# Two pauses of a recurrence, and the shape of the last token tile in a down projection (one Trainium2 core)

## The chip, the cores and the metric

The kernel runs on one core of one Trainium2 chip. The metric is device time in microseconds (us) of one launch. The engines are called by the short names of the profile: PE is TensorE (matmul), PEld its weight loads, DVE is VectorE, ACT is ScalarE, POOL is GpSimd, SP is SyncE, which here issues most of the DMA transfers.

## The reference

One layer of a hybrid backbone is computed twice: for 128 prompt tokens, and for 512 sample tokens that also read cached context (keys, values, recurrent states). The model width is 1024, the inner width of the feed-forward part 2816. Everything is float32.

```python
def token_mixers(h, lw, ...):
    proj = h @ lw['w_in']                      # 13 pieces, each 256 wide
    y_a = a_b * dwconv3(a_c * a_x, ...)
    y_b, s_f, s_b = hgrn2_bidir(b_q, b_ff, b_fb, b_i, b_g, ...)   # gated linear recurrence, both directions
    y_c = neighbourhood_attention(...)         # for the prompt: context_attention
    y_d = chunk_gmlp(d_u, d_v, ...)
    merged = g_a * (y_a @ w_br_a) + g_b * (y_b @ w_br_b) + g_c * (y_c @ w_br_c) + g_d * (y_d @ w_br_d)
    return merged @ lw['w_o'], kh, vh, s_f, s_b

def trunk_layer(x, cvec, lw, ...):
    mod = silu(cvec) @ lw['w_ada'] + lw['b_ada']                  # adaLN: sh1, sc1, g1, sh2, sc2, g2
    h = rmsnorm(x, norm1_g) * (1 + sc1) + sh1
    x = x + g1 * token_mixers(h)
    h = rmsnorm(x, norm2_g) * (1 + sc2) + sh2
    return x + g2 * conv_ffn(h)                # (silu(g) * a) @ w_down, a and g from dwconv3(h @ w_up)

y_prompt, y_sample = rmsnorm(xp, final_norm_g), rmsnorm(xs, final_norm_g)
```

The change touches the order of `hgrn2_bidir`'s work and the product with `w_down`, with the residual and the final norm behind it.

## The kernel before, in words

**Tiles.** The 640 tokens are five tiles of 128, four of samples and one of the prompt. Nearly all matrix products go through split numbers: a float32 operand is cut into a high and a low part, and a product is three matmuls (high by high, high by low, low by high). TensorE's stream is thus a long row of weight loads and matmuls with 320 or 512 moving columns. For the weights the high part is made by ScalarE (`act`, L310) and the low part by VectorE (L311).

**Who sets the order.** The program is written out in Python by an emitter that keeps a planner's clock, `now[0]`. Each stage of the main stream (`tick(us)`) adds its estimated length to that clock, and then resumes every background job whose due time has come. A background job is a Python generator: the recurrence `hgrn` (started behind the query section, with a slack factor of 1.3), the attention, the gMLP, the adaLN column steps `ada_cols`. At `yield x` a job is put off by x times its slack factor, counted from the clock as it stood before that step. Inside a step `pe(us)` adds the length of the matmuls that the step itself emits. Where an instruction is passed to `tc.keep_in_program_order`, its engine keeps it in the written order; between the others a scheduler chooses the order on each engine.

**The recurrence.** `hgrn` works through seven levels (`for l in range(7)`, L508). At level l it forms the products between neighbouring blocks of 2^l tokens. From level 1 on each level has two bursts, `par` 0 and 1, one for each half of the partitions: for levels 1 to 5 a burst is ten tokens' pieces i by four groups g, 40 products, written as 80 matmuls of 64 rows by 32 columns in the profile (L526), with `pe(0.18)` behind each piece. Between the bursts stands a pause (`yield 0.4`, L537), behind the level the updates of the running products (L545, L549) and a closing pause (`yield HD[1]`, L550, 5). While the bursts run, the main stream is the input projection (L362), 320 columns to a matmul. Levels 0 to 4 write into one buffer, which at the end of level 4 is copied out by ScalarE (L541).

**The down projection.** It works in two halves of the output columns (`nh`), 512 columns each, and in 11 steps (`kk_`) of 256 rows of `w_down`. `down_prep` makes the weight parts and the activations' parts of a step, `down_tile` its matmuls (L1795): for each of the five token tiles two row blocks by three products. Each tile has an accumulator in PSUM. In the second half the steps 8, 9 and 10 are held back and done together, tile by tile, so that each tile's output can follow while the next tile is computed. Before the change the last token tile (t = 4, the prompt) of the second half is computed in two halves of 256 columns in all 11 steps, each in an accumulator of its own.

`down_out` (L1799 to L1832) takes a finished accumulator to the output: VectorE multiplies by the gain g2 (L1806) and adds the residual (L1809); ScalarE squares with a running sum (L1812 in the first half, L1817 in the second); VectorE joins the sums of squares (L1818); GpSimd takes the root (`pow`, L1822); ScalarE scales the first 512 columns (L1824), VectorE the last 512 (L1825), and SyncE sends the row out (L1827). None of these is pinned by `keep_in_program_order`.

Of the kernel before, what the change touches and what calls it, by code (L numbers as in the profile page):

```python
# [15 lines left out]

P = 128
HD = [4, 5, 2.1, 7, 2.2, 1.4, 1.5, 5, 2.0, 2, 11]
OUTS = 1
NPAIR = 22  # L20
BRIDGE = 4
LORD = "0 8 w00 w10 w20 1 9 2 10 3 11 w01 w11 w21 4 5 12 13"
# [45 lines left out]
def tile_step(ctx: ExitStack, tc: tile.TileContext, a: dict, outs: list, dbg=None):  # L68
# [54 lines left out]
    def nm(s):  # L123
        cnt[0] += 1
        return f"{s}_{cnt[0]}"
# [321 lines left out]
    def hgrn():  # L447
# [51 lines left out]
        for l in range(7):  # L499
            B = 1 << l  # L500
            e_, x_ = blk(kk[:, 0], B), blk(kk[:, 1], B)
            r_, p_ = blk(qq[:, 0], B), blk(qq[:, 1], B)
            f_, g_ = blk(ff[:, 0], B), blk(ff[:, 1], B)
            nb = 1280 // (2 * B)
            if l == 0:
                m = yield from along(near)
                vec.copy_predicated(nat, lmask[:, 0, :].unsqueeze(1).to_broadcast([P, 20, 32]), bc(m))

            W = 64 if l == 6 else 32
            ns = 320 // W  # L510
            for s0, par in ([(s_, r) for s_ in range(0, 10, ns) for r in range(2)] if l else ()):
                b = slice(64 * par, 64 * par + 64)
                m = pm()
                for i in range(s0, s0 + ns):
                    for g in range(P // W):
                        d, t0 = (0, W * g) if l < 5 else (1 - g % 2, W * (g ^ 1))
                        t0 += (i % 5) * P
                        k0 = i * P + W * g
                        rhs = qq[b, d, i // 5, t0:t0 + W]
                        if l < 5:  # L520
                            lhs = kl[b, k0:k0 + W]
                            rhs = bass.AP(rhs.tensor, rhs.offset,
                                          [list(rhs.ap[0]), [2 * B, 16 // B], [1280 + B, 2], [1, B]])
                        else:
                            lhs = f2(kk[:, g % 2])[b, k0:k0 + W]
                        mm(m[W * g:W * g + W, (i - s0) * W:(i - s0 + 1) * W], lhs, rhs,  # L526
                           start=True, stop=True, tile_position=(64 * par, W * g))
                    pe(0.18)
                mv = m[:, 0:ns * W].rearrange("p (i t) -> p i t", t=W)
                if l < 5:  # L530
                    vec.copy_predicated(near_at[:, par], lmask[:, l, :].unsqueeze(1).to_broadcast([P, 10, 32]), mv)
                else:
                    for g in range(P // W):
                        c = slice(W * g, W * g + W)
                        act(at[c, par, s0:s0 + ns, W * (g ^ 1):W * (g ^ 1) + W], mv[c], AF.Copy)
                if par == 0:
                    yield 0.4  # L537
            if l == 4:
                for g in range(4):
                    c = slice(32 * g, 32 * g + 32)  # L540
                    act(at[c, :, :, c].rearrange("p r i t -> p (r i) t"), nat[c], AF.Copy)  # L541
            ups = ((e_[:, :, 0, :], f_[:, :, 1, 0:1]), (x_[:, :, 1, :], g_[:, :, 0, 0:1]),
                   (p_[:, :, 1, :], f_[:, :, 0, 0:1]), (r_[:, :, 0, :], g_[:, :, 1, 0:1]))
            for i, (dst, mul) in enumerate(ups):
                vec.tensor_tensor(dst, dst, mul.to_broadcast([P, nb, B]), ALU.mult)  # L545
                if i == 1 and l < 4:
                    kl = keys(l + 1)
            fa = ff.rearrange("p d n t -> p (d n t)").rearrange("p (n j i) -> p n j i", j=2, i=B)
            vec.tensor_tensor(fa[:, :, 0, 0], fa[:, :, 0, 0], fa[:, :, 1, 0], ALU.mult)  # L549
            yield HD[1]  # L550
        vec.tensor_copy(tot, ff.rearrange("p d n (t s) -> p d n t s", s=P)[:, :, :, :, 0])
        R["tots"] = True

# [1211 lines left out]
    def down_tile(nh, kk_, ws):  # L1765
# [7 lines left out]
        if kk_ == 0:  # L1773
            if nh == 0:
                g0, g1, m0 = pg(), pg(), pm()
                acc[0] = [g0[:, 0, :], g0[:, 1, :], g1[:, 0, :], g1[:, 1, :], m0]
            else:
                ms = [pm(), pm(), pm()]
                g0, g1 = pg(), pg()
                acc[1] = ms + [g0[:, 0, :], g1[:, 0, :], pm()]  # L1780
        batch = [ws]
        if nh == 1 and kk_ >= 8:
            acc.setdefault("hold", []).append(ws)
# [2 lines left out]
            batch = acc["hold"]  # L1786
        last = kk_ == 10
        for t in range(5):

            halves = ((0, 256), (256, 512)) if nh == 1 and t == 4 else ((0, 512),)  # L1790
            for c0, c1 in halves:
                for bi, (w, sl) in enumerate(batch):
                    for k in range(2):
                        for i, (hx, hw) in enumerate(((0, 0), (0, 1), (1, 0))):
                            mm(acc[nh][t + c0 // 256][:, 0:c1 - c0], sl[k][hx][:, t * P:(t + 1) * P], w[:, hw, k, c0:c1],  # L1795
                               start=(kk_ == 0 and k == 0 and i == 0),
                               stop=(last and bi == len(batch) - 1 and k == 1 and i == 2))
                        tick(0.65 * (c1 - c0) / 512)
                if last:  # L1799
                    down_out(nh, t, c0, c1)  # L1800

    def down_out(nh, t, c0, c1):
        v = 0 if t < 4 else 1
        cs = slice(nh * 512 + c0, nh * 512 + c1)
        tmp = gp.tile([P, 512], F32, tag="gt", name=nm("dt"))[:, 0:c1 - c0]
        vec.tensor_tensor(tmp, acc[nh][t + c0 // 256][:, 0:c1 - c0], grows["g2"][:, v, cs], ALU.mult)  # L1806
        xs = x2[t][:, cs]
        fg = fx["fn"][:, 1280:2304]
        vec.tensor_tensor(xs, xs, tmp, ALU.add)  # L1809
        q = st3[:, t:t + 1]  # L1810
        if nh == 0:
            act(tmp, xs, AF.Square, accum_out=q)  # L1812
            pool.tensor_tensor(xs, xs, fg[:, cs], ALU.mult)
            vec.tensor_scalar(q, q, 1.0 / D, EPS, ALU.mult, ALU.add)
            return
        q1 = st3[:, 8 + t:9 + t]
        act(tmp, xs, AF.Square, accum_out=q1)  # L1817
        vec.scalar_tensor_tensor(q, q1, 1.0 / D, q, ALU.mult, ALU.add)  # L1818
        if c1 < 512:
            return  # L1820
        r_ = st3[:, 16 + t:17 + t]
        pool.tensor_tensor(r_, q, neghalf[:, 0:1], ALU.pow)  # L1822
        dst = y_sample[0, t * P:(t + 1) * P, :] if t < 4 else y_prompt[0]
        act(x2[t][:, 0:512], x2[t][:, 0:512], AF.Copy, scale=r_)  # L1824
        vec.scalar_tensor_tensor(x2[t][:, 512:], x2[t][:, 512:], r_, fg[:, 512:], ALU.mult, ALU.mult)  # L1825
        if OUTS == 1 or t < 4:
            nc.sync.dma_start(dst, x2[t])  # L1827
        else:
            nc.sync.dma_start(dst[:, 0:512], x2[t][:, 0:512])
            nc.scalar.dma_start(dst[:, 512:], x2[t][:, 512:])  # L1830

    for nh in range(2):  # L1832
        for kk_ in range(11):
# [339 lines left out]
```

## Time and profile before

| what | value |
|---|---|
| median of 3 runs (lowest to highest) | 1027.42 us (1027.24 to 1028.08) |
| the profiled execution's own time | 1028.79 us |
| its span, first to last instruction | 1026.9 us |
| mean granted TensorE clock | 0.996 of full speed |
| busy: VectorE | 792.3 us, 77% of the span, 1300 instructions |
| busy: ScalarE | 535.5 us, 52% of the span, 927 instructions |
| moved by DMA | 177.87 MB, mean 173 GB/s |

A row of the timeline has the start in us from the span's start, the length in us, the engine, the line of the kernel, the operation, the output and inputs by the program's names with partitions x elements, and how many such instructions in a row it stands for (x73). In brackets stands the idle time of the engine just before, in us, and what ended it; "issue" is idle time in which the engine waited for nothing that the profile shows. Matmuls overlap, so the start to start distance is the time that one costs. A row of the table of waits gives who waited for what, then the total, the number of times and the longest. A row of the table of stretches gives for a stretch A:B its length, then the busy time and the number of instructions of each engine, the mean granted TensorE clock (PEclk), the busy share of the DMA engines and the rate moved. A row of a queue gives packets, MB, and the share of the 16 DMA engines' time.

### The profile page before, as it was taken

What the parts mean: (1) busy time and instruction counts of PE and PEld (TensorE: products, weight loads), DVE (VectorE), ACT (ScalarE), POOL (GpSimd) and SP (SyncE); (2) the same over time, 40 slices, a digit from 0 to 9 for tenths busy, and PEclk for the clock granted to TensorE, in tenths of its full rate; (3) what the DMA queues carried; (4) which work ended last, traced back from release to release, by engine and by line L of the source; (5) the groups of instructions that cost most, each with busy time, mean ns of one, the idle gap of its engine ahead of it and who ended that gap; (6) DMA issues with size and microseconds to landing.
All of it is one profiled execution on the core that took longest, in us unless ns stands there. A gap on an engine that the chain in (4) does not pass through costs nothing.

```text
span 1026.9 us, 18833 instructions
## 1 busy us (share of the span) xinstructions
PE 1013.4 (99%) x7620; PEld 957.8 (93%) x7620; DVE 792.3 (77%) x1300; ACT 535.5 (52%) x927; POOL 106.2 (10%) x149
## 2 busy tenths in 40 slices
PE   8999999999999999999999999999999999999997
PEld 6899999999899999999998899999999999888886
DVE  6658889679965676767768879998888887797634
ACT  6642343444444444544544567777777776633332
POOL 1000010313100000000010111111112211001101
PEclk9999999999999999999999999999999999999999
DMA  9864333598562413323179584765555669974212
GB/s 354 319 220 127 125 108 121 137 270 268 121 205 78 137 69 103 127 79 103 41 276 359 200 333 109 192 167 150 149 150 149 156 161 274 366 248 149 89 35 103
DMA packets 55927, 177.87 MB, mean 173 GB/s; under 512 B 8192, under 2 KB 14624, under 8 KB 53280
## 3 DMA queue, kind: packets, MB, share of 16 engines
q1 hardware_dynamic: 45008, 140.60, 39.5%
q0 software_dynamic: 10832, 36.06, 14.7%
q8 instruction: 60, 0.98, 0.4%
q14 instruction: 27, 0.22, 0.1%
HBM read 134.93 MB, written 25.46 MB: 156 GB/s over the span
## 4 chain that ended last, share of the span: by engine, by line
PE 96%; DMA 1%; ACT 1%; DVE 1%; issue 1%; SPq 0%; POOL 0%; POOLq 0%; DVEq 0%; ACTq 0%
PE g L1464 19%; PE g L362 17%; PE m L1108 17%; PE g L1795 8%; PE m L1795 6%; PE g L1121 5%; PE m L1464 4%; PE m L1248 3%; PE g L920 2%; PE g L1248 2%; PE m L148 2%; PE g L148 1%; PE m L526 1%; PE m L1459 1%; DMA A<-in_w_ada_dram 1%; PE m L851 1%
## 5 line engine op out<-in xcount | busy, mean ns | idle before, releaser
L362 PE MATMUL g<-XH,w 128*128 128x320 f32 x704 | 171.9, 319 | 0.0
L362 PEld LDWEIGHTS g<-XH,w 128*128 128x128 f32 x704 | 121.6, 190 | 2.2 <-issue 1.2
L362 PE MATMUL g<-XL,w 128*128 128x320 f32 x352 | 109.8, 312 | 0.0
L362 PEld LDWEIGHTS g<-XL,w 128*128 128x128 f32 x352 | 66.9, 190 | 0.3 <-issue 0.2
L311 DVE TENSOR_TENSOR w<-raw,w 128x1024 fp32r<-128x1024 f32 x34 | 41.5, 1222 | 21.4 <-ACT w L310 15.2
L1108 PE MATMUL m<-XH,w 128*128 128x320 f32 x224 | 52.5, 309 | 0.0
L1795 PE MATMUL g<-w,XH 128*128 128x512 f32 (+1 forms) x216 | 47.6, 373 | 0.0
L310 ACT ACTIVATE w<-raw 128x1024 fp32r<-128x1024 f32 x34 | 35.7, 1050 | 21.3 <-PE g L1248 9.9
L1795 PEld LDWEIGHTS g<-w,XH 128*128 128x128 f32 x216 | 38.4, 188 | 7.6 <-ACT XH L1758 0.3
L148 DVE SCALAR_TENSOR_TENSOR X<-MG,p2t,X 128x641 f32<-128x641 f32 x44 | 38.9, 885 | 4.3 <-ACT X L148 3.4
L148 DVE SCALAR_TENSOR_TENSOR X<-X,p2t,X 128x641 f32<-128x641 f32 x44 | 38.9, 885 | 1.9 <-ACT X L148 1.0
L1795 PE MATMUL g<-w,XL 128*128 128x512 f32 (+1 forms) x180 | 39.8, 372 | 0.0
L148 ACT ACTIVATE w<-raw 128x1024 fp32r<-128x1024 f32 (+3 forms) x46 | 38.2, 850 | 2.9 <-DMA raw<-in_w_in_dram 2.0
L1795 PE MATMUL m<-w,XH 128*128 128x512 f32 (+1 forms) x180 | 39.7, 368 | 0.0
L1464 PE MATMUL g<-XL,w 128*128 128x320 f32 x240 | 38.6, 310 | 0.0
L1464 PE MATMUL g<-XL,C 128*128 128x320 f32 x240 | 38.4, 309 | 0.0
L1795 PEld LDWEIGHTS g<-w,XL 128*128 128x128 f32 x180 | 32.3, 188 | 6.5 <-DVE dt L1806 0.4
L1108 PEld LDWEIGHTS m<-XH,w 128*128 128x128 f32 x224 | 38.3, 188 | 0.0
L1464 PEld LDWEIGHTS g<-XL,w 128*128 128x128 f32 x240 | 36.0, 188 | 0.5 <-ACT MG L148 0.3
L1464 PEld LDWEIGHTS g<-XL,C 128*128 128x128 f32 x240 | 35.9, 188 | 0.4 <-ACT MG L148 0.4
L1795 PEld LDWEIGHTS m<-w,XH 128*128 128x128 f32 x180 | 31.3, 189 | 5.3
L1108 PE MATMUL m<-XL,w 128*128 128x320 f32 x112 | 34.6, 309 | 0.0
(546 smaller groups left out, 2764.5 us busy)
## 6 DMA issues: line engine op xcount, KB each, us to landing
raw<-in_w_up_dram SPq DMA_DIRECT2D x30, 512.0 KB, 5.2
raw<-in_w_gp_dram SPq DMA_DIRECT2D x21, 640.0 KB, 3.9
raw<-in_w_down_dram SPq DMA_DIRECT2D x22, 512.0 KB, 4.0
raw<-in_w_in_dram SPq DMA_DIRECT2D x19, 512.0 KB, 4.1
H<-in_w_adt_dram SPq DMA_DIRECT2D x16, 512.0 KB, 4.3
actd<-X POOLq DMA_DIRECT2D x22, 320.5 KB, 5.5
X<-in_w_adt_dram SPq DMA_DIRECT2D x10, 512.0 KB, 4.4
upd<-XL SPq DMA_DIRECT2D x4, 1280.0 KB, 6.5
```

The source lines that it names most:

```text
L148: r = f(*args, **kw)
L310: act(w[0], raw, AF.Copy)
L311: vec.tensor_tensor(w[1], raw, w[0].bitcast(F32), ALU.subtract)
L362: mm(o, w[:, h, k0 + k, :], r(k)[:, s], start=(k == 0 and i == 0), stop=(k == kt - 1 and i == 2))
L526: mm(m[W * g:W * g + W, (i - s0) * W:(i - s0 + 1) * W], lhs, rhs, start=True, stop=True, tile_position=(64 * par, W * g))
L851: mm(mo[64 * hh_:64 * hh_ + 64, 0:P], v, ptt[(u + hh_) % 3][:, j * P:(j + 1) * P], start=(j == 0), stop=(j == 2))
L920: mm(o, x(kx)[:, ts], w[:, h, k, :], start=(kx == 0 and i == 0), stop=(kx == 7 and i == 2))
L1108: mm(o, w[:, k, :], x[:, k, :], start=(first and k == 0 and j == 0), stop=(k == 3 and j == 2), skip_group_check=True)
L1121: mm(pb[:, c, 0:HC], w[:, h + k, :], y[:, x, k, s], start=(k == 0 and j == 0), stop=(k == 1 and j == 2))
L1248: mm(m, mh[k // 2][:, hx, k % 2, t * P:(t + 1) * P], wo[q][:, hw, k % 2, :], start=(k == 0 and i == 0), stop=(k == 7 and i == 2))
L1464: z = mm(o, w[:, k, :], x[:, k, :], start=(first and k == 0 and j == 0), stop=(k == 3 and j == 2), skip_group_check=True)
L1795: mm(acc[nh][t + c0 // 256][:, 0:c1 - c0], sl[k][hx][:, t * P:(t + 1) * P], w[:, hw, k, c0:c1], start=(kk_ == 0 and k == 0 and i == 0), st ...
```

## The change

In the recurrence, the pause between the two bursts of level 4 is 1.6 instead of 0.4, and the closing pause behind level 4 is 3.8 instead of 5. The other levels keep theirs.

In the second half of the down projection, the last token tile is computed whole (512 columns) for steps 0 to 7, in one accumulator. After step 7 that accumulator is emptied: multiplied by the gain, and added to the residual (`gained`, `added`). The held steps 8 to 10 are computed in two halves of 256 columns as before, in two fresh accumulators (`acc["halves"]`).

`down_out` is cut into pieces (`gained`, `added`, `down_root`, `down_store`), and for the last two halves VectorE's order is written out: the first half's multiply and add; the output of token tile 3; then the second half's multiply, the join of the first half's sum of squares, the second half's add, its square, and its join. The second half's square moves from ScalarE to VectorE. The root is written in place. The constant `OUTS`, which chose between two ways of sending the last row out, is gone; the way that it chose stays.

```diff
@@ -16,7 +16,6 @@
 
 P = 128
 HD = [4, 5, 2.1, 7, 2.2, 1.4, 1.5, 5, 2.0, 2, 11]
-OUTS = 1
 NPAIR = 22
 BRIDGE = 4
 LORD = "0 8 w00 w10 w20 1 9 2 10 3 11 w01 w11 w21 4 5 12 13"
@@ -534,7 +533,7 @@
                         c = slice(W * g, W * g + W)
                         act(at[c, par, s0:s0 + ns, W * (g ^ 1):W * (g ^ 1) + W], mv[c], AF.Copy)
                 if par == 0:
-                    yield 0.4
+                    yield 1.6 if l == 4 else 0.4
             if l == 4:
                 for g in range(4):
                     c = slice(32 * g, 32 * g + 32)
@@ -547,7 +546,7 @@
                     kl = keys(l + 1)
             fa = ff.rearrange("p d n t -> p (d n t)").rearrange("p (n j i) -> p n j i", j=2, i=B)
             vec.tensor_tensor(fa[:, :, 0, 0], fa[:, :, 0, 0], fa[:, :, 1, 0], ALU.mult)
-            yield HD[1]
+            yield HD[1] - (1.2 if l == 4 else 0)
         vec.tensor_copy(tot, ff.rearrange("p d n (t s) -> p d n t s", s=P)[:, :, :, :, 0])
         R["tots"] = True
 
@@ -1775,9 +1774,11 @@
                 g0, g1, m0 = pg(), pg(), pm()
                 acc[0] = [g0[:, 0, :], g0[:, 1, :], g1[:, 0, :], g1[:, 1, :], m0]
             else:
+
                 ms = [pm(), pm(), pm()]
                 g0, g1 = pg(), pg()
-                acc[1] = ms + [g0[:, 0, :], g1[:, 0, :], pm()]
+                acc[1] = ms + [g0[:, 0, :], g0[:, 1, :]]
+                acc["halves"] = [g1[:, 0, :], pm()]
         batch = [ws]
         if nh == 1 and kk_ >= 8:
             acc.setdefault("hold", []).append(ws)
@@ -1786,48 +1787,80 @@
             batch = acc["hold"]
         last = kk_ == 10
         for t in range(5):
-
-            halves = ((0, 256), (256, 512)) if nh == 1 and t == 4 else ((0, 512),)
-            for c0, c1 in halves:
+            halved = last and nh == 1 and t == 4
+            for ci, (c0, c1) in enumerate(((0, 256), (256, 512)) if halved else ((0, 512),)):
+                ps = (acc["halves"][ci] if halved else acc[nh][t])[:, 0:c1 - c0]
                 for bi, (w, sl) in enumerate(batch):
                     for k in range(2):
                         for i, (hx, hw) in enumerate(((0, 0), (0, 1), (1, 0))):
-                            mm(acc[nh][t + c0 // 256][:, 0:c1 - c0], sl[k][hx][:, t * P:(t + 1) * P], w[:, hw, k, c0:c1],
-                               start=(kk_ == 0 and k == 0 and i == 0),
-                               stop=(last and bi == len(batch) - 1 and k == 1 and i == 2))
+                            first = (kk_ == 0 or halved and bi == 0) and k == 0 and i == 0
+                            end = k == 1 and i == 2 and bi == len(batch) - 1
+                            mm(ps, sl[k][hx][:, t * P:(t + 1) * P], w[:, hw, k, c0:c1],
+                               start=first, stop=end and (last or nh == 1 and t == 4 and kk_ == 7))
                         tick(0.65 * (c1 - c0) / 512)
                 if last:
-                    down_out(nh, t, c0, c1)
-
-    def down_out(nh, t, c0, c1):
-        v = 0 if t < 4 else 1
+                    down_out(nh, t, c0, c1, ps)
+        if nh == 1 and kk_ == 7:
+            gained(1, 4, 0, 512, acc[1][4])
+            added(1, 4, 0, 512)
+
+    keep_ = tc.keep_in_program_order
+    prods = {}
+
+    def gained(nh, t, c0, c1, ps):
+
+        tmp = prods[t] = gp.tile([P, 512], F32, tag="gt", name=nm("dt"))[:, 0:c1 - c0]
+        return vec.tensor_tensor(tmp, ps, grows["g2"][:, 0 if t < 4 else 1, nh * 512 + c0:nh * 512 + c1], ALU.mult)
+
+    def added(nh, t, c0, c1):
+        xs = x2[t][:, nh * 512 + c0:nh * 512 + c1]
+        return vec.tensor_tensor(xs, xs, prods[t], ALU.add)
+
+    def down_out(nh, t, c0, c1, ps):
         cs = slice(nh * 512 + c0, nh * 512 + c1)
-        tmp = gp.tile([P, 512], F32, tag="gt", name=nm("dt"))[:, 0:c1 - c0]
-        vec.tensor_tensor(tmp, acc[nh][t + c0 // 256][:, 0:c1 - c0], grows["g2"][:, v, cs], ALU.mult)
         xs = x2[t][:, cs]
-        fg = fx["fn"][:, 1280:2304]
-        vec.tensor_tensor(xs, xs, tmp, ALU.add)
-        q = st3[:, t:t + 1]
+        q, q1, q2 = (st3[:, i + t:i + t + 1] for i in (0, 8, 16))
+        join = lambda x: vec.scalar_tensor_tensor(q, x, 1.0 / D, q, ALU.mult, ALU.add)
         if nh == 0:
-            act(tmp, xs, AF.Square, accum_out=q)
-            pool.tensor_tensor(xs, xs, fg[:, cs], ALU.mult)
+            gained(nh, t, c0, c1, ps)
+            added(nh, t, c0, c1)
+            act(prods[t], xs, AF.Square, accum_out=q)
+            pool.tensor_tensor(xs, xs, fx["fn"][:, 1280:2304][:, cs], ALU.mult)
             vec.tensor_scalar(q, q, 1.0 / D, EPS, ALU.mult, ALU.add)
-            return
-        q1 = st3[:, 8 + t:9 + t]
-        act(tmp, xs, AF.Square, accum_out=q1)
-        vec.scalar_tensor_tensor(q, q1, 1.0 / D, q, ALU.mult, ALU.add)
-        if c1 < 512:
-            return
-        r_ = st3[:, 16 + t:17 + t]
-        pool.tensor_tensor(r_, q, neghalf[:, 0:1], ALU.pow)
+        elif t < 4:
+            gained(nh, t, c0, c1, ps)
+            added(nh, t, c0, c1)
+            act(prods[t], xs, AF.Square, accum_out=q1)
+            join(q1)
+            down_root(t)
+            if t < 3:
+                down_store(t)
+        elif c0 == 0:
+
+            keep_(gained(nh, t, c0, c1, ps))
+            keep_(added(nh, t, c0, c1))
+            down_store(3)
+            keep_(act(prods[t], xs, AF.Square, accum_out=q1))
+        else:
+            keep_(gained(nh, t, c0, c1, ps))
+            keep_(join(q1))
+            keep_(added(nh, t, c0, c1))
+            keep_(vec.scalar_tensor_tensor(prods[t], xs, 1.0, xs, ALU.mult, ALU.mult, accum_out=q2))
+            keep_(join(q2))
+            down_root(4)
+            down_store(4)
+
+    def down_root(t):
+        pool.tensor_tensor(st3[:, t:t + 1], st3[:, t:t + 1], neghalf[:, 0:1], ALU.pow)
+
+    def down_store(t):
         dst = y_sample[0, t * P:(t + 1) * P, :] if t < 4 else y_prompt[0]
-        act(x2[t][:, 0:512], x2[t][:, 0:512], AF.Copy, scale=r_)
-        vec.scalar_tensor_tensor(x2[t][:, 512:], x2[t][:, 512:], r_, fg[:, 512:], ALU.mult, ALU.mult)
-        if OUTS == 1 or t < 4:
-            nc.sync.dma_start(dst, x2[t])
-        else:
-            nc.sync.dma_start(dst[:, 0:512], x2[t][:, 0:512])
-            nc.scalar.dma_start(dst[:, 512:], x2[t][:, 512:])
+        xs = x2[t][:, 512:]
+        act(x2[t][:, 0:512], x2[t][:, 0:512], AF.Copy, scale=st3[:, t:t + 1])
+        m = vec.scalar_tensor_tensor(xs, xs, st3[:, t:t + 1], fx["fn"][:, 1280 + 512:2304], ALU.mult, ALU.mult)
+        if t > 2:
+            keep_(m)
+        nc.sync.dma_start(dst, x2[t])
 
     for nh in range(2):
         for kk_ in range(11):
```

## The prediction, made before the changed kernel was run

> **What bounds the kernel now.** I read the page's head first, then the chain that ended last, then TensorE's waits, then the stretches that the change touches.
>
> ```profile
> span 1026.9 us, 18833 instructions
> ...
> PE 1013.4 (99%) x7620; PEld 957.8 (93%) x7620; DVE 792.3 (77%) x1300; ACT 535.5 (52%) x927; POOL 106.2 (10%) x149
> ...
> PE 96%; DMA 1%; ACT 1%; DVE 1%; issue 1%; SPq 0%; POOL 0%; POOLq 0%; DVEq 0%; ACTq 0%
> ```
>
> TensorE is busy in 99% of the span and is 96% of the chain that ended last. An edit therefore counts if it shortens TensorE's own stream, if it takes away one of that engine's few waits, or if it shortens what follows the last matmul. The profiled execution took 1028.79 us, 1.89 beyond its span of 1026.9; the median of the runs is 1027.42, which is 1.37 less. I work in the profiled span and put the difference on the median. A difference under 0.2% (2.05 us) I call the same, about what a measurement of this kernel can tell from no change.
>
> TensorE's waits hold one row at the recurrence's matmul line, L526:
>
> ```profile
> PE m L526 <- issue: 1.1, 1, 1.1
> ```
>
> It is one wait, "issue", so no engine's semaphore ended it. The timeline and the table of stretches show where it is, and that it costs more than itself:
>
> ```profile
> 132.42 0.31 PE L362 MATMUL g<-XL,w 128*128 128x320 f32 x1
> ...
> 132.86 0.31 PE L362 MATMUL g<-XL,w 128*128 128x320 f32 x1
> ...
> 136.04 0.82 PE L526 MATMUL m<-C,E 64*32 64x32 f32 x73
> 138.00 0.26 PE L526 MATMUL m<-C,E 64*32 64x32 f32 x7 [1.14 <-issue]
> ...
> 139.25 0.47 PE L362 MATMUL g<-XL,w 128*128 128x320 f32 x1
> ...
> 140.05 0.47 PE L362 MATMUL g<-XL,w 128*128 128x320 f32 x1
> ```
>
> ```profile
> core 0: us, PE busy (x) PEld busy (x) DVE busy (x) ACT busy (x) POOL busy (x), PEclk, DMA share, GB/s
> 902.39:922.79 20.40, 20.40 (x92) 16.90 (x91) 18.45 (x33) 7.11 (x11) 0.00 (x0) 1.00 0.73 240
> 954.47:995.87 41.40, 41.40 (x217) 35.65 (x216) 19.73 (x22) 13.90 (x18) 0.00 (x0) 1.00 0.20 64
> ...
> 138.19:141.88 3.69, 3.69 (x21) 3.69 (x15) 3.53 (x7) 2.94 (x4) 0.00 (x0) 0.54 0.35 127
> 210.00:314.00 104.00, 104.00 (x769) 96.87 (x769) 84.02 (x169) 49.78 (x88) 17.89 (x22) 1.00 0.68 199
> ```
>
> This is level four's second burst of 80 small matmuls. After 73 of them TensorE stands still for 1.14 us. Then three 320-column matmuls take 0.80 us (139.25 to 140.05) instead of 0.44 (132.42 to 132.86), for 3.69 us at a granted clock of 0.54. 3.69 us at 0.80 per three are 13.8 matmuls, which at full pace take 2.03 us, so 1.66 are lost. The place costs 1.14 + 1.66 = **2.8 us**, the largest single loss that the change goes near.
>
> By the Trainium skill ("TensorE: Matmul & The Clock Gate", Part 1: The HAM clock gate) the clock falls after an idle window of about 3.4 us. Here 1.14 us did it, so the trace differs; by the page's rule only 1.14 would be at stake here.
>
> What does the "issue" wait for? The queue rows suggest the fetching of TensorE's own instructions:
>
> ```profile
> q8 instruction: 60, 0.98, 0.4%
> ```
>
> ```profile
> q8 instruction: 1, 0.02, 1.5%
> ```
>
> The first row is the whole execution, the second the transfers between 134 and 138 us. TensorE issues 7620 matmuls and 7620 weight loads, 15240 in all. 0.98 MB over these is 64 bytes each, and 15240 in 60 packets is about 256 to a packet. One packet falls beside the stall. The burst's 73 pairs, 146 instructions, were issued in 0.82 us, where the large matmuls take 18.8 us for a packet's 256 (128 pairs at 0.147). I take it that the burst used up its instructions before the next packet was in; this is inferred.
>
> **Part 1, the recurrence's pauses.** The emitter that interleaves the recurrence with the projection takes the time of a step from before the step. Level four's first burst itself advances the planner's clock by 10 x 0.18 for its matmuls and 0.52 for rows emitted with it: 2.32 in its units. A pause of 1.6, with the slack factor 1.3, is 2.08, less than that; 0.4 is 0.52. Both have run out when the emitter looks again, so the second burst is due at the same moment. The order of the built program says the same: TensorE's stream is identical through both bursts of level four, and the other engines' too. So **the longer pause does nothing, and the stall's place is not touched: 0** (if it were, rival B).
>
> The shorter closing pause (3.8 for 5, times 1.3: 1.56 units earlier) does act. Level five's two bursts move ahead of 12 matmuls of 320 columns, 12 x 0.147 = 1.76 us. They stand here, with no wait on their rows:
>
> ```profile
> 145.20 0.89 PE L526 MATMUL m<-C,B 64*32 64x32 f32 x80
> ...
> 146.66 0.89 PE L526 MATMUL m<-C,B 64*32 64x32 f32 x80
> ```
>
> The same matmuls run in another order, so TensorE's work is unchanged. From level five on the recurrence runs 1.8 to 2.7 us ahead of the projection; it is not on the chain there, and being earlier wins nothing. Later, a few attention steps are issued 1.2 to 2.7 us later, two reads of weights swap places on SyncE's queue, and one more adaLN column step falls into the attention. That step costs VectorE two of these pairs and a small operation, about 2.7 us:
>
> ```profile
> 239.70 1.22 DVE L262 SCALAR_TENSOR_TENSOR junk<-H,S 128x1024 bf16<-128x1024 f32 x1
> 240.84 0.08 DVE L262 DVE_READ_ACCUMULATOR junk<-H,S 128x1 f32 x1
> ```
>
> In 210 to 314 us VectorE is busy 84.02 of 104 us (81%), and TensorE never idles. The 20 us that VectorE has free cover the 2.7, unless they stand in the wrong place. Bounds: −0.5 (a small wait of TensorE goes) to +2.7 (all of it is uncovered). I take **+0.15**, near the covered end, because that row shows no idle TensorE.
>
> **Part 2, the whole last tile.** A step of the first column half has five whole tiles, one of the second has four and two halves.
>
> ```profile
> 902.39 5.60 PE L1795 MATMUL g<-w,XH 128*128 128x512 f32 x24
> ...
> 909.19 5.60 PE L1795 MATMUL g<-w,XL 128*128 128x512 f32 x24
> ```
>
> ```profile
> 954.47 2.24 PE L1795 MATMUL g<-w,XH 128*128 128x512 f32 x12
> ...
> 961.37 2.24 PE L1795 MATMUL g<-w,XH 128*128 128x512 f32 x12
> ```
>
> 909.19 − 902.39 = 6.80 us; 961.37 − 954.47 = 6.90. The long stretches agree: 20.40 for three steps, 41.40 for six. Six pairs of halves thus cost 0.10 us over six whole tiles, and eight steps change: **−0.80 us**, in TensorE's own stream, at full clock and with no wait. I allow 0.7 to 0.9. The work is otherwise equal: the order has 48 matmuls and 48 weight loads fewer.
>
> The Trainium skill ("TensorE: Matmul & The Clock Gate", Back-to-back issue gap) gives N/2.4 + 2.5 ns for a matmul of N columns, so a pair of halves costs 2.5 ns more than a whole. By that estimate 48 pairs are 0.12 us, not 0.80; the measured steps decide against it, and I keep 0.80.
>
> The accumulator is now also emptied after step 7, a multiply and an add of 512 columns on VectorE, priced by the rows of tile 0:
>
> ```profile
> 999.96 1.23 DVE L311 TENSOR_TENSOR w<-raw,w 128x1024 fp32r<-128x1024 f32 x1 [4.79 <-ACT w L310]
> ...
> 1002.97 0.69 DVE L1806 TENSOR_TENSOR dt<-m,S 128x512 f32<-128x512 f32 x1 [1.79 <-PE m L1795]
> 1003.70 0.69 DVE L1809 TENSOR_TENSOR X<-X,dt 128x512 f32<-128x512 f32 x1
> ```
>
> It is 1.4 us. Queued behind it on VectorE is the last step's low weight half (L311, 999.96 to 1001.19, after 4.79 us idle), and its first reader is the held batch's matmuls. The idle 4.79 us cover most of it; if the two meet, L311 starts about 0.4 us late. Bounds 0 and +0.4; I take **+0.05**, since tile 0's high products come first.
>
> **Part 2, the tail.** Before:
>
> ```profile
> 1015.73 1.60 PE L1795 MATMUL g<-w,XH 128*128 128x256 f32 x12
> ...
> 1017.37 0.42 DVE L1806 TENSOR_TENSOR dt<-g,S 128x256 f32<-128x256 f32 x1 [0.74 <-PE g L1795]
> ...
> 1017.83 0.42 DVE L1809 TENSOR_TENSOR G<-G,dt 128x256 f32<-128x256 f32 x1
> 1017.88 1.60 PE L1795 MATMUL m<-w,XH 128*128 128x256 f32 x12
> ...
> 1018.69 0.75 DVE L1825 SCALAR_TENSOR_TENSOR X<-X,st,F 128x512 f32<-128x512 f32 x1 [0.44 <-POOL st L1822]
> ...
> 1019.85 0.16 DVE L1818 SCALAR_TENSOR_TENSOR st<-st 128x1 f32<-128x1 f32 x1 [0.40 <-ACT dt L1817]
> 1019.92 0.42 DVE L1806 TENSOR_TENSOR dt<-m,S 128x256 f32<-128x256 f32 x1
> 1020.37 0.43 DVE L1809 TENSOR_TENSOR G<-G,dt 128x256 f32<-128x256 f32 x1
> ...
> 1021.43 0.16 DVE L1818 SCALAR_TENSOR_TENSOR st<-st 128x1 f32<-128x1 f32 x1 [0.63 <-ACT dt L1817]
> ...
> 1023.08 0.33 SPq L1827 DMA_DIRECT2D out_dram<-G  x1
> ```
>
> The last matmul ends at E = 1017.88 + 1.60 = 1019.48. VectorE then waits until E+0.37 for ScalarE's square of the first half, joins it, and multiplies the second half only from E+0.44. Then the add, ScalarE's square, and the second join at E+1.95. In the changed kernel the multiply comes first: for the first half it began 0.04 after its matmuls (1017.33 to 1017.37), so E+0.04. The join fits between it and the add, as at 1017.37 to 1017.83, so the add is at E+0.50 and the square, now VectorE's, at E+0.95. The square's length is not shown for this shape: 0.42 is the 256-column multiply, 0.61 half of L262's 1.22, each with the 0.08 for reading the accumulator. I take 0.43 plus about 0.05, nearest to the operation of the same size: second join at E+1.43. That is **−0.5** (bounds −0.3 to −0.6). What is late next is the same chain: root, last multiply, output transfer. The cover is thin: token tile 3's multiply ends at 1019.44, 0.08 ahead of the new multiply's start.
>
> **Sum.** −0.80 + 0.05 − 0.5 + 0.15 = **−1.1 us**: the span becomes 1025.8, the median 1027.42 − 1.1 = **1026.3**. With the bounds of the parts (the reorder from −0.5 to +0.8; beyond that it is rival D) it is 1025.4 to 1027.6.
>
> **The rivals.**
> B, the change does what it says at level four. If the stall hangs on something other than the stream ahead of it (when a transfer happens to land), it may go: −2.8 − 1.1 = −3.9, 1023.5. Against it: the instructions up to there are the same, in the same order.
> C, the slower side: the stall's like appears at level five. These 320 instructions, 1.76 us earlier, may end where the next packet is not in yet. Price 2.8 as at level four: −1.1 + 2.8 = +1.7, 1029.1; and over 2.05 if it stands still 0.4 longer. It decides where a packet lands later than the burst reaches the packet's first instruction. Counting 256 instructions to a packet from the stall on, I find some 3 us between the moved bursts and their limits, against it.
> D, the extra adaLN step is not covered in the attention: +1.0 to +2.7 in place of +0.15, so 1027.2 to 1028.9, about 1028. Against it: 20 us of VectorE free and TensorE without a wait in 210 to 314.
> A further way, part 2 hidden altogether, I don't give a case: TensorE's stream is the chain there.
>
> **How the numbers follow.** Forecast 0.66, B 0.13, C 0.10, D 0.11. Faster by over 0.2% (below 1025.37): B and 0.04 of the forecast, whose bounds are not hard, 0.17. Slower by over 0.2% (above 1029.47): 0.06 of C and 0.02 of D, 0.08. The rest, 0.75, is within. The range from 1023.3 to 1028.9 leaves out C and a part of B, under 0.2.
>
> **What would show it.** Level four's stall still there with its 1.14 us and half clock (else B). L526's level-five rows without an "issue" wait (else C). No TensorE wait in 210 to 314 (else D). Steps of 6.80 us in the second column half. L1806 of the last half within 0.1 us of the last matmul's end, and the last join about 1.43 us after that end instead of 1.95. A span under 1024 or over 1028 would make the forecast wrong.

## The result and the profile after

| | median | lowest to highest | executions |
|---|---|---|---|
| before | 1028.05 us | 1027.24 to 1029.95 | 10 |
| changed | 1030.16 us | 1028.38 to 1032.89 | 10 |

The ratio is 1.0021, with a 95% interval from 1.0012 to 1.003: about 2.1 us slower, where 1.1 us faster was forecast, and above the top of the forecast range (1028.9). The profiled execution of the changed kernel took 1031.38 us with a span of 1029.6; that of before 1028.79 with 1026.9. Lines of the changed kernel up to the down projection have numbers one lower than before (L525 is the old L526).

The page's head, and the shares of the chain:

```profile
span 1029.6 us, 18747 instructions
...
PE 1013.7 (98%) x7572; PEld 955.6 (93%) x7572; DVE 794.3 (77%) x1304; ACT 535.8 (52%) x925; POOL 104.5 (10%) x149
...
PE 91%; DVE 3%; DMA 2%; issue 1%; ACT 1%; SPq 0%; POOL 0%; POOLq 0%; DVEq 0%; ACTq 0%
```

TensorE's busy time is almost unchanged (1013.7 for 1013.4), yet the span is 2.7 us longer, and VectorE, 1% of the chain before, is 3% of it. So TensorE stands and waits somewhere that it didn't. Its waits say where:

```profile
PE m L147 <- DMA A<-in_w_ada_dram: 1.8, 2, 1.3
PE m L525 <- issue: 1.7, 1, 1.7
PE g L147 <- DVE F L147: 1.6, 1, 1.6
PE m L850 <- DVE B L835: 1.5, 1, 1.5
PE m L833 <- DVE X L830: 1.1, 2, 0.9
```

The rows for L850 and L833 are new; both are matmuls of the attention that wait for VectorE. Together they are 2.6 us. The longest single wait of the two in the timeline:

```profile
286.20 0.22 DVE L829 RECIPROCAL ast<-ast 128x1 f32<-128x1 f32 x2
...
288.49 0.69 DVE L147 TENSOR_TENSOR S<-raw,raw 128x512 f32<-128x512 f32 x1 [2.07 <-DMA raw<-in_w_gp_dram]
289.10 0.55 DVE L835 COPY B<-m 128x384 f32<-128x384 f32 x1
...
289.70 0.54 PE L850 MATMUL m<-B,X 128*64 128x128 f32 x5 [1.47 <-DVE B L835]
```

VectorE stands for 2.07 us at an operation that waits for a load; the copy for which TensorE waits is queued behind it. The wait at level four is 0.5 us longer than before, and so is the one for the first weights (A<-in_w_ada_dram, 1.8 for 1.3).

The down projection does what was worked out. Its steps in the second column half, from the timeline:

```profile
958.32 2.88 PE L1798 MATMUL g<-w,XH 128*128 128x512 f32 x12
961.04 4.24 PE L1798 MATMUL m<-w,XH 128*128 128x512 f32 x18
965.12 2.88 PE L1798 MATMUL g<-w,XH 128*128 128x512 f32 x12
```

A step is 965.12 − 958.32 = 6.80 us (6.90 before). And the tail:

```profile
1021.06 1.60 PE L1798 MATMUL m<-w,XH 128*128 128x256 f32 x12
...
1022.70 0.42 DVE L1813 TENSOR_TENSOR dt<-m,S 128x256 f32<-128x256 f32 x1 [0.49 <-PE m L1798]
1023.04 0.15 DVE L1823 SCALAR_TENSOR_TENSOR st<-st 128x1 f32<-128x1 f32 x1
1023.15 0.42 DVE L1817 TENSOR_TENSOR G<-G,dt 128x256 f32<-128x256 f32 x1
1023.61 0.42 DVE L1848 SCALAR_TENSOR_TENSOR dt<-G 128x256 f32<-128x256 f32 x1
1023.96 0.08 DVE L1848 DVE_READ_ACCUMULATOR dt<-G 128x1 f32 x1
1024.08 0.16 DVE L1823 SCALAR_TENSOR_TENSOR st<-st 128x1 f32<-128x1 f32 x1
```

The last matmul ends at 1022.66. The multiply starts 0.04 us later (0.44 before), and the second join, at 1024.08, 1.42 us later (1.95 before); it was forecast at 1.43.

The gain of the second part is there, then, and the loss lies in the recurrence's part. The experiments take the two apart, and then look for what in the first part costs, and for what the "issue" wait is.

### The profile page after: what moved, and what is told of

Read it like the earlier page. It is cut to its first block, busy times and chain, and to the rows that moved or that the text cites. A ratio compares the mean times of both kernels' runs of the same rounds, so it can differ in the third digit from the quotient of the medians.

```text
span 1029.6 us, 18747 instructions
## 1 busy us (share of the span) xinstructions
PE 1013.7 (98%) x7572; PEld 955.6 (93%) x7572; DVE 794.3 (77%) x1304; ACT 535.8 (52%) x925; POOL 104.5 (10%) x149
## 4 chain that ended last, share of the span: by engine, by line
PE 91%; DVE 3%; DMA 2%; issue 1%; ACT 1%; SPq 0%; POOL 0%; POOLq 0%; DVEq 0%; ACTq 0%
PE g L1463 19%; PE m L1107 17%; PE g L361 14%; PE g L1798 8%; PE m L1798 6%; PE g L1120 5%; PE m L1463 4%; PE m L1247 3%; PE g L919 2%; PE g L1247 2%; PE m L147 2%; PE g L147 1%; PE m L525 1%; PE m L1458 1%; DMA A<-in_w_ada_dram 1%
## 5 line engine op out<-in xcount | busy, mean ns | idle before, releaser
L1798 PE MATMUL g<-w,XH 128*128 128x512 f32 (+1 forms) x216 | 50.2, 385 | 0.0
L1798 PE MATMUL g<-w,XL 128*128 128x512 f32 (+1 forms) x180 | 42.4, 386 | 0.0
L1798 PE MATMUL m<-w,XH 128*128 128x512 f32 (+1 forms) x156 | 36.4, 381 | 0.0
L322 ACT ACTIVATE w<-raw 128x1024 fp32r<-128x1024 f32 (+1 forms) x22 | 24.3, 1104 | 20.7 <-PE g L361 7.9
```

Source lines behind the costliest of these rows:

```text
L322: high = lambda: act(w[:, 0], raw, AF.Copy)
L1798: mm(ps, sl[k][hx][:, t * P:(t + 1) * P], w[:, hw, k, c0:c1], start=first, stop=end and (last or nh == 1 and t == 4 and kk_ == 7))
```

## The experiments

Each kernel is compared with the kernel before on the same chip; its ratio is to those runs.

**The recurrence's part alone.**

```diff
-                    yield 0.4
+                    yield 1.6 if l == 4 else 0.4
-            yield HD[1]
+            yield HD[1] - (1.2 if l == 4 else 0)
```

> The recurrence's part of the change alone (both pauses; the down projection as before). Theory A: the loss comes from this part, by VectorE and a load running late in the attention, about 2.6 us of TensorE waiting on L834 and L851 in the profile, and the other part is worth -1.3; then this run is 3.0 to 3.6 us slower than before, near 1031.4, with those waits in its trace. Theory B: this part is neutral, as predicted (+0.15), and the difference of the two profiles is the chance length of the level-four stall (1.14 us in one, 1.66 in the other) and something in the down projection; then it is within 0.5 us of before.

Measured: 1031.41 us, ratio 1.0036 (1.0024 to 1.0047), so 3.7 us slower (2.5 to 4.8). Theory B falls. Theory A has the place right, but not the sum of the waits: the profile has 1.6 us of them (1.4 on L851, 0.2 on L834) for the 2.6 expected. It was taken of the fastest of the eight executions, 1029.93 us. VectorE's and TensorE's rows at the longest wait, from the timeline of this kernel:

```profile
283.60 0.21 DVE L830 RECIPROCAL ast<-ast 128x1 f32<-128x1 f32 x2
...
285.81 0.69 DVE L148 TENSOR_TENSOR S<-raw,raw 128x512 f32<-128x512 f32 x1 [2.00 <-DMA raw<-in_w_gp_dram]
286.42 0.55 DVE L836 COPY B<-m 128x384 f32<-128x384 f32 x1
...
287.03 0.54 PE L851 MATMUL m<-B,X 128*64 128x128 f32 x5 [1.40 <-DVE B L836]
```

The operation S<-raw,raw prepares the first gate pair's weights and has nothing to do with the attention. It stands ahead of the attention's copy L836 in VectorE's queue, waits 2.00 us for its load, and TensorE waits 1.40 us for the copy behind it. These are the changed kernel's rows at 288 us over again. In the kernel before, that operation comes at 294.08, behind all of these copies, without a wait.

**The down projection's part alone** (both pauses as before).

> The down projection's part alone (both pauses as before). Theory A: the terms of the prediction hold here, -0.80 for the whole tile, -0.5 for the tail, +0.05: 1.2 to 1.4 us faster than before, near 1026.7, steps of 6.80 us, and no wait on L833 or L850. Theory B: the part is worth nothing or costs, because what it frees is waited for elsewhere: 1028 or more.

Measured: 1028.23 us beside 1028.16 for before, ratio 0.9993 (0.9984 to 1.0002). No wait on L833 or L850 in the profile. The steps and waits are as theory A has them, but the median, 1028.23, lies where theory B put it (1028 or more). The size was not settled by this run: its executions fall in two groups, 1026.3 to 1026.5 and 1027.4 to 1028.7, of which more below; the last pair of runs measures it better.

**The extra adaLN step put back.** The change lets column 31's step fall behind the start of the recurrence's output.

```diff
-            while "hgrn_out" in R and "hgrn_done" not in R:
+            while f != 30 and "hgrn_out" in R and "hgrn_done" not in R:
```

> The changed kernel, except that the adaLN step that fell into the attention is emitted before the recurrence's output again, as in the kernel before (column 31 doesn't wait there). Theory A1: this one extra step on VectorE (2.7 us) makes the attention late; then the waits on L833 and L850 go or fall under 0.5 us in all, and the time is near 1027. Theory A2: what counts is that the attention's steps themselves are issued later against the projection, and the load behind which VectorE's queue stands at 288 us; then the waits stay, 1.5 to 2.6 us, and the time is 1029.5 to 1030.5.

Measured: 1033.75 us, ratio 1.0053 (1.0041 to 1.0066), 3.3 us above the changed kernel by the ratios. Theory A1 falls: other waits appear, 1.56 us for VectorE's L830 at 260 us and 2.75 us for ScalarE's L957 at 291 us. The rows ahead of them show the same kind of cause as in the changed kernel, an operation that stands first in its engine's queue and waits for a load:

```profile
252.17 1.22 DVE L261 SCALAR_TENSOR_TENSOR junk<-H,S 128x1024 bf16<-128x1024 f32 x1 [1.41 <-DMA H<-in_w_adt_dram]
...
260.26 0.52 PE L833 MATMUL m<-cst,X 128*128 128x128 f32 x3 [1.56 <-DVE X L830]
...
288.45 0.42 ACT L147 ACTIVATE H<-raw 128x256 fp32r<-128x256 f32 x1 [2.10 <-DMA raw<-in_w_gp_dram]
...
291.03 0.64 PE L361 MATMUL g<-XH,w 128*128 128x320 f32 x1 [2.75 <-ACT gt L957]
```

A2's number, 1029.5 to 1030.5, was missed too; of its waits that on L833 is there (2.0 us in all), that on L850 is not. So this run moved more than the one step, and doesn't price the step by itself.

**Level five ahead, everything from level six on back.**

```diff
-            yield HD[1] - (1.2 if l == 4 else 0)
+            yield HD[1] + {4: -1.2, 5: 1.6}.get(l, 0)
```

> The changed kernel with level five's closing pause longer by 1.6: level five's bursts stay where the change put them, and from level six on the recurrence is back at its old place; VectorE's order in the attention is then that of the down projection's part alone. Theory A: the loss of the recurrence's part comes from what is ordered differently behind level five (attention, adaLN steps, loads); then it is gone here, no wait on L833 or L850, and the time is that of the down projection's part alone, 1027 to 1028.2. Rival: level five's new place itself costs (fetching of instructions, VectorE's updates there); then it is 1029.5 or more.

Measured: 1027.0 us beside 1028.96, ratio 0.9986 (0.9977 to 0.9994). Neither L833 nor L850 waits. Theory A holds: level five's new place costs nothing, and the loss is what is ordered differently behind it.

**The sums on GpSimd.** In the changed kernel the four sums of the first gate pair's weights go to GpSimd.

```diff
-        ovec.tensor_tensor(s[:, 0], b11, b12, ALU.add)
+        e = ovec if p_ else opool
+        e.tensor_tensor(s[:, 0], b11, b12, ALU.add)
...
```

> The changed kernel with the four sums of the first gate pair's weights (128x512 each) on GpSimd instead of VectorE. In the changed kernel the first of them stands in VectorE's queue ahead of the attention's copy L835 and waits 2.07 us for its load. Theory A3: that queue position costs the 1.47 us of TensorE's wait on L850; then this wait goes and the run is 1.2 to 1.8 us faster than the changed kernel, near 1028.5. Rival: the attention is late anyway, because its steps are issued later, and the wait shows again at the next copy; then it stays within 0.5 us of the changed kernel, near 1030.

Measured: 1029.64 us, ratio 1.0002 (0.9993 to 1.0011), beside 1.0021 for the changed kernel: 1.9 us better. The wait on L850 is gone, as A3 has it, and the gain is just above its 1.2 to 1.8 us (its 1028.5 was missed, but the kernel before was 0.9 us slower here too than beside the changed kernel). The wait on L833 stays (0.23 and 1.11 us), and against the run above, which has neither, 1.6 us are left.

**The stall at level four, by position: 7 warm-up matmuls more** in the kernel before (`WARM = 107`).

> The kernel before with 7 more warm-up matmuls (107 for 100, 14 more instructions of TensorE ahead of everything). Theory F, instructions fetched in packets of 256: the stop in level four's second burst moves by 7 pairs to the front, so that the burst's rows read x66 and x14 instead of x73 and x7. Rival G, something that comes at its moment: the stop stays after 73, or falls elsewhere, or there is none.

```profile
135.20 0.89 PE L526 MATMUL m<-C,E 64*32 64x32 f32 x80
136.67 0.77 PE L526 MATMUL m<-C,E 64*32 64x32 f32 x66
138.97 0.43 PE L526 MATMUL m<-C,E 64*32 64x32 f32 x14 [1.53 <-issue]
```

The stop came after 66 of 80, 7 earlier: theory F. (One execution, 1035.19 us, with a wait of 2.4 us in the down projection, for VectorE's L1806, that is at most 0.3 us in every other run; its time isn't used.) It is the 1747th matmul of TensorE's stream after which it stops here, in the kernel before and in the changed one.

**18 warm-up matmuls fewer** in the down projection's part alone (`WARM = 82`).

> The down projection's part alone with 18 warm-up matmuls fewer (82 for 100, 36 instructions less ahead of everything; the order behind them is unchanged). Theory F: the end of the fetched instructions falls 18 pairs later, behind level four's burst, among the projection's large matmuls, which take 1.6 us for the 22 instructions that lie between; the packet, which came 1.1 to 1.7 us too late, is then just in time: no issue wait at L525, or one under 0.3 us, no half clock behind it, and 1.2 us or more under the down projection's part, near 1026.5 with a scatter as small as with the longer pause. Rival G: the wait stays, and the time is that of the part alone, near 1028.

Measured: 1026.4 us, ratio 0.9977 (0.9967 to 0.9988). Level four's burst now runs through its 80 without a stop, and the median is as theory F has it; the scatter, 1025.3 to 1028.61, isn't as small as it says. And a wait of 0.93 us came up in a place that was not expected, level one:

```profile
110.32 0.89 PE L525 MATMUL m<-C,D 64*32 64x32 f32 x80
111.69 0.74 PE L525 MATMUL m<-C,D 64*32 64x32 f32 x62
113.36 0.37 PE L525 MATMUL m<-C,D 64*32 64x32 f32 x18 [0.93 <-issue]
```

It stops there after the 1108th matmul. Matmuls and weight loads together, that is 2216 instructions; the other stop is after 3494. The distance is 1278. The trace also has 25 instructions of TensorE's sequencer ahead of the one stop and 27 ahead of the other, and with these it is 1280, five packets of 256. So the two stops lie on one grid, and which burst is hit depends on the number of instructions ahead of it.

**A pause that acts.** The down projection's part, and

```diff
-                    yield 0.4
+                    yield 4 if l == 4 else 0.4
-            yield HD[1]
+            yield HD[1] - (2.5 if l == 4 else 0)
```

> The down projection's part with a pause of 4 between level four's bursts, which is long enough to act (24 of the projection's matmuls lie between the bursts in place of 3), and a closing pause of 2.5 so that level five stands where it stood before. Theory F: the stall at level four is TensorE running out of fetched instructions; with 3 us between the bursts the packet is there in time, so the wait (1.14 us) and the half clock behind it (1.66) go: 2.8 us below the down projection's part alone, near 1023.9. Rival G: the stall hangs on something that comes at its moment whatever TensorE does; then an issue wait of over 1 us stays near 137 us, and the time is near 1026.7.

Measured: 1026.09 us, ratio 0.9976 (0.9968 to 0.9985), all executions between 1025.55 and 1026.68. No issue wait at L525, granted clock 1.00 throughout 130 to 150 us:

```profile
130.00:150.00 20.00, 20.00 (x431) 18.88 (x429) 16.44 (x31) 10.64 (x19) 6.55 (x6) 1.00 0.35 108
```

The wait is gone, as theory F has it, and the rival falls. But F's 1023.9 was missed by 2.2 us; by the time alone the rival's 1026.7 is nearer.

**The down projection's part without the stall**: the pause of 4 in the kernel before, and in the down projection's part, on one chip.

> The kernel before with the pause of 4 between level four's bursts and a closing pause of 2.5; the down projection as before. With the stall gone in this run and in the next, their difference is the down projection's part without the scatter of the half clock. Theory: the terms -0.80, -0.5 and +0.05 stand, so this run is 1.1 to 1.4 us slower than the next one, near 1027.3 where the next is near 1026.1. Rival: the part's gain is smaller than its terms (0.7, as the down projection's part alone against the kernel before showed): under 0.9.

> The down projection's part with the pause of 4 once more, on the same chip as the run before it, for that difference: 1.1 to 1.4 us faster than it, near 1026.1; rival: less than 0.9.

Measured: 1027.49 and 1026.33 us, 11 executions each: 1.16 us apart (0.7 to 1.7, by drawing again from the executions). That agrees with the sum of the prediction's terms for this part (−1.25); the rival (under 0.9) lies inside the interval too and is not excluded. Against the kernel before on this chip the first of the two is 0.8 us faster (ratio 0.9992, 0.9983 to 1.0), which is what the pause alone is worth there.

**A pause just long enough.** The down projection's part with a pause of 2.3 and a closing pause of 4.4.

> The down projection's part with a pause of 2.3 between level four's bursts, the first length that moves the second burst by two steps of the planner: 6 matmuls, 0.88 us later; the closing pause keeps level five at its old place. Theory F: the packet comes when it came, so the wait shrinks by what lies between, from 1.1 to 1.7 us down to 0.3 to 0.8, and the half clock behind it is rarer: 0.5 to 1 us below the part alone. Rival G: the wait keeps its length or is gone altogether.

```profile
134.62 0.89 PE L525 MATMUL m<-C,E 64*32 64x32 f32 x80
136.96 0.77 PE L525 MATMUL m<-C,E 64*32 64x32 f32 x67
138.33 0.32 PE L525 MATMUL m<-C,E 64*32 64x32 f32 x13 [0.60 <-issue]
```

Measured: 1025.45 us beside 1028.74, ratio 0.9972 (0.9963 to 0.9981): 3.3 us faster in the medians, the best of all. Six large pairs now stand in front of the burst that stood behind it, and the stop comes after 67 instead of 73, which is again the 1747th matmul; the wait is 0.60 us, inside theory F's 0.3 to 0.8. The time isn't: by the ratios it is 2.1 us below the part alone, for the 0.5 to 1 expected, and its median is 0.9 us below that of the run with the pause of 4, which has no stop at all. No run here shows why.

## Why the prediction was wrong, and where it was right

**The step that failed is the reorder of part 1**, put at +0.15 "near the covered end, because that row shows no idle TensorE", with +2.7 as the far bound. Measured alone, part 1 is +3.7 (2.5 to 4.8), and with everything from level six on put back at its old place the loss is gone. Two things were wrong with the term.

The free 20 us of VectorE in 210 to 314 us are a sum over the stretch and say nothing of an instruction at a given place. The kernel before had almost no margin there: its copy-and-multiply chain ended just as TensorE came to it (timeline of before):

```profile
256.59 0.41 DVE L831 TENSOR_SCALAR X<-X,ast 128x384 f32<-128x384 f32 x1
...
257.14 0.52 PE L834 MATMUL m<-cst,X 128*128 128x128 f32 x3
```

The multiply ends at 257.00, and TensorE starts at 257.14. A delay of VectorE beyond 0.14 us would show there.

And the pricing followed the extra instructions (the adaLN step), not the order. The prediction had seen the swaps on SyncE's queue and named them, but priced no instruction that waits on a load at the head of VectorE's queue. That was the largest single item: 1.4 to 1.5 us of TensorE for an operation that isn't the attention's. Rival D was right on the place, VectorE in the attention. Its cause, the extra adaLN step, isn't borne out: with the step put back the kernel was slower still, though by loads at other places. Its price, 1027.2 to 1028.9, was too low.

Point by point:

- The longer pause does nothing: right. With 0.4 put back in the changed kernel the built program is the same, instruction for instruction, on every engine. It would have to be over 2.32 / 1.3 = 1.79 to act; 2.3 acts.
- The stall stays: right, and rival B falls. It stands after 73 of 80 as before, for 1.66 us.
- It is the fetching of TensorE's instructions: only inferred then. Three runs have moved it through the number of instructions ahead of it, 7 pairs for 7, 6 for 6, and by five packets. The trace also keeps the times of the 16 KB packets on TensorE's instruction queue: one landed at 136.58 us in the kernel before, and TensorE went on at 138.00; in the changed kernel it landed at 137.25, and TensorE went on at 138.66. In all ten profiles with a stop TensorE goes on 1.3 to 1.5 us after such a landing, early or late. I take it as shown.
- Its price of 2.8 us, which the rivals B and C use, was mis-sized. The wait is there in each profile of that order (1.1 to 1.7 us), the half clock (1.66) in five of these eight: the granted clock in 130 to 150 us was 0.91 in the profiles of before and of the changed kernel, for example, and 1.00 in those of the recurrence's part and of the down projection's part alone. With the pause of 4 the time fell by 1.7 us in the down projection's part (ratio 0.9976 against 0.9993) and by 0.8 in the kernel before, not by 2.8.
- Rival C, a stall at level five: no issue wait there in any run with the shorter closing pause; the extra wait of the run with 82 warm-up matmuls came at level one.
- Whole tile −0.80, tail −0.5, eviction +0.05: right, by the steps of 6.80 us and the second join at 1.42 us after the last matmul; TensorE shows no wait for the eviction. Together they measure −1.16 (−0.7 to −1.7). With the +3.7 of part 1 that makes +2.5, beside the +2.1 of the changed kernel.

What stays open is most of the other 1.6 us of the recurrence's part. With the sums on GpSimd and without the wait on L850 they are still there, and the profile puts 1.3 us of them on L833. Of these, 0.23 us near 233 us stand in every profile of the moved order but that with the adaLN step put back, and in none of the old order. The other 1.1 us lead to one more load. GpSimd's two additions that read it (X<-in_rpbe_dram) came late in the changed kernel, and VectorE's small operations beside them took longer than before. Before:

```profile
246.05 0.73 POOL L806 TENSOR_TENSOR B<-X 128x256 f32<-128x256 f32 x1 [2.71 <-DMA X<-in_rpbe_dram]
...
250.94 1.00 DVE L694 SCALAR_TENSOR_TENSOR MG<-MG,cst 128x511 f32<-128x511 f32 x2
251.86 0.74 DVE L696 SCALAR_TENSOR_TENSOR MG<-MG,cst 128x511 f32<-128x511 f32 x1
```

Changed:

```profile
252.87 1.49 DVE L693 SCALAR_TENSOR_TENSOR MG<-MG,cst 128x511 f32<-128x511 f32 x2
253.34 1.62 POOL L805 TENSOR_TENSOR B<-X 128x256 f32<-128x256 f32 x2 [8.11 <-DMA X<-in_rpbe_dram]
254.28 1.23 DVE L695 SCALAR_TENSOR_TENSOR MG<-MG,cst 128x511 f32<-128x511 f32 x1
...
260.05 0.52 PE L833 MATMUL m<-cst,X 128*128 128x128 f32 x3 [0.86 <-DVE X L830]
```

VectorE loses 0.98 us on these three, and TensorE, with its margin of 0.14 us, waits 0.86. That the additions slow VectorE down is inferred from the rows that stand side by side. The two loads took 8.3 us from issue to landing here and 4.6 before. In the four profiles in which they took 8.0 to 8.6 us this wait is 0.86 to 1.19 us; where they took 6.1 and 6.2 us it is 0.1 and 0.4; in six with 4.3 to 5.5 us there is none. (The thirteenth is the run with the adaLN step put back, whose wait has the cause shown there.) Two of the four, those with 107 warm-up matmuls and with the pause of 4 in the kernel before, have the attention ordered as before. So the wait is partly chance at a place without margin; how much of it the change causes wasn't settled, since no run moved that load.

The Trainium skill ("TensorE: Matmul & The Clock Gate", Part 1: The HAM clock gate) has the hardware watch a free-running window, and the clock fall after an idle one of about 3.4 us. Stops of 1.1 to 1.7 us were followed by it here, in five of eight profiles. That it comes in some executions only, by the trace's clock records from 0.2 us before the stop's end to 1.6 us after it, would fit a window that runs free of the program; no run here tests it.

## What to carry to other kernels

Before a pause or a due time is counted as an edit, ask whether the step before it is already longer: here 1.6 and 0.4 were the same program. When an edit moves a background job, read the new order of the engine that feeds TensorE next to the loads its instructions wait for, and look for the rows of before in which TensorE just makes it; the idle share of a stretch is no cover. A wait for "issue" in a burst of small matmuls can be tested cheaply: add a few instructions far ahead of it, and see whether it moves by as many.

## What the runs showed of the hardware that was not expected

Where a point of the grid of 256 instructions (128 pairs) falls, TensorE goes on only some time after a packet has landed: at the 1108th and the 1747th matmul, in all thirteen profiles, it goes on 1.3 us or more after the last landing. Two bursts of 80 small pairs close together use up a packet's 128 pairs in 2.0 us, and may come to the point earlier; then TensorE stands, 0.6 to 1.7 us in the profiles here. At level one of the kernel before, the point is passed at 112.32 us without a stop, 1.75 us after the landing at 110.56. A change of a few warm-up matmuls moves the stop from one burst to another.

Much of the scatter of the kernel fits the half clock behind such a stop. Of the 24 executions of the kernel before that stand beside the first four runs, 12 of the 13 with a mean clock of 0.998 took 1026.75 to 1028.24 us, and the six with 0.996 took 1028.78 to 1029.94; 3.69 us at 0.54 lower the mean by 0.0017. Where in an execution without a profile the clock was low isn't shown. With the pause of 4, and no stop, 22 executions of the down projection's part lay between 1025.55 and 1027.05. Of 11 executions of the kernel before with that pause, ten lay between 1026.66 and 1028.25 and one at 1029.91, so something else scatters too. In the changed kernel the half clock set in 1.5 us after the stop had ended, for 3.65 us (table of stretches, changed kernel):

```profile
140.15:143.80 3.65, 3.65 (x17) 3.65 (x16) 3.58 (x8) 2.34 (x4) 1.21 (x1) 0.54 0.00 1
```
